# A hybrid encoder trunk on one core: four edits in the order of the first FFN

## The chip, the cores and the metric

The kernel runs on one core of one Trainium2 chip. A core has TensorE (matmuls; PE in the profile, with PEld for its weight loads), VectorE (DVE), ScalarE (ACT), GpSimd (POOL) and SyncE (SP, which issues transfers). TensorE reads its operands from on-chip memory (SBUF) and writes to accumulator banks (PSUM); a bank has to be read out before it is used again. The metric is the device time in microseconds (us) of one execution. The time before is 2467.57 us, the median of 3 runs (2467.53 to 2467.99).

## The reference, cut to what matters

Two layers, each a half-step FFN, a mixer (short convolution and attention) and a second half-step FFN, on 640 tokens of width 1024; all in float32.

```python
def _rmsnorm(x, g):
    y = xf * lax.rsqrt(jnp.mean(xf * xf, axis=-1, keepdims=True) + EPS)
    return y * g

def _swiglu(h, w_gu, w_down):              # w_gu: 1024 x 5632, w_down: 2816 x 1024
    g, u = jnp.split(h @ w_gu, 2, axis=-1)
    return (jax.nn.silu(g) * u) @ w_down

for l in range(2):
    x = x + 0.5 * _swiglu(_rmsnorm(x, norm_ffn1[l]), w_ffn1_gu[l], w_ffn1_down[l])
    x = x + mixer(_rmsnorm(x, norm_mix[l]))
    x = x + 0.5 * _swiglu(_rmsnorm(x, norm_ffn2[l]), w_ffn2_gu[l], w_ffn2_down[l])
```

The change touches only the first FFN of the first layer ("a0" in the code).

## The kernel before, in words

Everything is kept transposed: x is eight tiles of 128 channels by 640 tokens, and a matmul takes 128 x 128 weights and 320 tokens (one half of the tokens, `t1` or `t2`). To keep float32 accuracy with the faster matmul type, every operand is split into a high part (`hi`, made by ScalarE as a cast to fp32r) and a low part (`lo` = value - hi, made by VectorE), and a product is three matmuls: hi x hi, lo x hi (of x) and hi x lo (of the weights). So each slab of weights (128 x 1024, tile `raw`) costs one cast on ScalarE (L369, `whi`) and one subtraction on VectorE (L375, `wlo`).

The norm's scale per token is not applied to x ahead of the products. The matmuls run on x times the gain; the sum of squares of x is built meanwhile (`square` on ScalarE, `add` on VectorE), summed over the channels by TensorE (`begun`, L552), turned into a root on ScalarE (L742) and spread over the partitions by TensorE again (`spread`, L571), which gives `rho`; the results of the products are multiplied by `rho` when they are read out of their banks.

**The opening** (`opening`, L755 on). The first four columns of gates are computed plainly: eight products `po` (gate and up of columns 0 to 3), eight blocks of x deep. For the first two products the loop over k (L770) brings in x block by block: `ex.plain(k)` splits x's block (for even k in two halves, L677 to L680; for odd k in one go, L668 and L669), and L774 and L775 split the piece of the first two weight slabs that has just landed. The two products fill two accumulators; there are only two such accumulators (each two banks), so the third product waits until the first is read out by `out(0)`, a copy on ScalarE (L795), and the fourth until `out(1)` (L803). A loop of eight squares and additions (L813) follows the matmuls in the text, and the two copies stand in it behind the fifth and the sixth square. Temporary tiles (squares, g and u) share four buffers.

**Seven products for four** (`gate_up`, L895 on). The later columns use sums and differences of weights and of x so that seven block products do the work of eight. A gate has four slabs s0 to s3; s1 is a sum that VectorE makes first (`source`, two additions on L298, then L369 and L375 split it). The closing work of a gate (`tail`, L1029) multiplies the gate by rho, makes the product g * u (`Pair.product`, L1059), splits it (`parts`) and so makes an operand for a later down product. It is put into a list and run later, at the place where the next unit calls it.

**The down products by rows** (`down_rows`, L1159 on). After gates 4 and 5 comes the first group of the down product of columns 0 to 3: accumulators A (for a and, in its second half of life, its sums), B and two single banks c. Seven matmul groups (`mul`) follow one another, and results are read out by `stage` (a copy on ScalarE, sent to x by an accumulating transfer on POOL, `send`) or by `take` (VectorE adds the bank to x, L1202). The last group (XT4) accumulates into A on top of what `take(a, ...)` has read, so it waits for that. In this first group the tail of gate 5 and the step "d1" (`place`, the three sums L1133 to L1136 of `Pair.rest`) stand near the start, ahead of the first `take`.

**The order.** From the start up to gate 6 the order on TensorE, VectorE and ScalarE is that of the text, written out by hand (`order(ORDERED)`, L1298); from gate 6 (L1304) only TensorE's is, and the scheduler may put work of VectorE and ScalarE from there into holes that it sees ahead. Transfers of weight slabs are issued on SP (L294); POOL issues some weight loans (`lent`, L277 and L278) and the accumulating transfers to x (L1197).

Of the kernel before, what the change touches and what calls it, by code (L numbers as in the profile page):

```python
# [12 lines left out]
AF = mybir.ActivationFunctionType  # L13
# [3 lines left out]
P = 128  # L17
# [169 lines left out]
def two(ps):  # L187
    return ps[:, :, :HT]


def halves(t):
    return t.rearrange("p (a b) -> p a b", a=2)
# [3 lines left out]
def trunk(ctx: ExitStack, tc: tile.TileContext, xin, wst, small, pbias, samplebias, kcache, vcache, gfin,  # L196
          yout, yrows, ko, vo, co):
    nc = tc.nc
    PE, DVE, ACT, POOL, SP = nc.tensor, nc.vector, nc.scalar, nc.gpsimd, nc.sync
# [21 lines left out]
    def acc(name):  # L221
        return banks["acc"].tile([P, 2, 512], F32, tag="acc", name=name)

    def att(name):
        return banks["att"].tile([P, 512], F32, tag="att", name=name)
# [4 lines left out]
    def tmp(name):  # L230
        return tp.tile([P, UW], F32, tag="t", name=name)[:, :T]
# [27 lines left out]
    raws, ready = [], []  # L259
# [113 lines left out]
    def flush(n=None):  # L373
        for lo, src, hi in pending[:n]:
            DVE.tensor_tensor(out=lo, in0=src, in1=hi.bitcast(F32), op=ALU.subtract)  # L375
        del pending[:n]
# [20 lines left out]
    def ahead():  # L397

        source(len(ready))
# [41 lines left out]
    def multiply(ps, ws, xs, first, last, seeded=False):  # L441
        (wh, wl), (xh, xl) = ws, xs
        for j, (w, x) in enumerate(((wh, xh), (wh, xl), (wl, xh))):
            for a in range(2):
                PE.matmul(ps[:, a, :HT], w, x[a] if isinstance(x, tuple) else x[:, a * HT : (a + 1) * HT],  # L445
                          start=first and j == 0 and not seeded, stop=last and j == 2,
                          skip_group_check=seeded)
# [43 lines left out]
    x = [xp.tile([P, T], F32, name=f"x{k}") for k in range(KT)]  # L491
    for k in range(KT):
# [4 lines left out]
        c = slice(k // 2 * 2 * P, (k // 2 + 1) * 2 * P)  # L497
# [86 lines left out]
    class Expand(Stats):  # L584
# [71 lines left out]
        def plain(self, m):  # L656

            kp, odd = divmod(m, 2)
            n = f"{self.name}_{kp}"
            g = sm[:, self.goff + m : self.goff + m + 1]  # L660

            def low(lo, src, hi):
                DVE.scalar_tensor_tensor(out=lo, in0=src, scalar=g, in1=hi.bitcast(F32),
                                         op0=ALU.mult, op1=ALU.subtract)

            if odd:
                hi, lo = (z[:, 3:5] for z in self.ops[kp])
                ACT.activation(hi, halves(x[m]), AF.Copy, scale=g)  # L668
                low(lo, halves(x[m]), hi)  # L669
                return tuple(tuple(z[:, a] for a in range(2)) for z in (hi, lo))  # L670
            hi, lo = (self.fp.tile([P, 7, HT], F32R, name=f"x{i}{n}", tag=f"x{i}{kp}") for i in ("hi", "lo"))
            self.ops.append((hi, lo))
            if kp % 2 == 0:
                self.side = [hp.tile([P, T], F32R, tag=f"h{i}", name=f"x2{i}{n}") for i in ("hi", "lo")]
            c = slice(kp % 2 * HT, (kp % 2 + 1) * HT)
            out = (hi[:, X11], self.side[0][:, c]), (lo[:, X11], self.side[1][:, c])
            for a, (h, l) in enumerate(zip(*out)):  # L677
                src = x[m][:, a * HT : (a + 1) * HT]
                ACT.activation(h, src, AF.Copy, scale=g)
                low(l, src, h)  # L680
            return out
# [73 lines left out]
    def opening(fp, name, goff, n, pairs, tails):  # L755

        ACT.copy(early, epst)
        ex = Expand(fp, name, goff)  # L760
        h = []
        for i in range(2):
            ready.append(tuple(wp.tile([P, CH], F32R, tag=f"w{t}", name=f"w{t}{i}", bufs=3) for t in ("hi", "lo")))

        idle, row = att("idle"), tmp("row")[:, :P]
        DVE.memset(row, 1.0)
        for i in range(WAKE):
            PE.matmul(idle[:, :P], ones.to_broadcast([P, P]), row, start=i == 0, stop=i == WAKE - 1)
        first = [acc(f"po{name}_{i}") for i in range(2)]
        for k in range(KT):  # L770
            h.append(ex.plain(k))
            c = slice(k // 2 * 2 * P, (k // 2 + 1) * 2 * P)
            raw, (whi, wlo) = raws[k % 2], ready[k % 2]
            ACT.copy(whi[:, c], raw[:, c])  # L774
            DVE.tensor_tensor(out=wlo[:, c], in0=raw[:, c], in1=whi[:, c].bitcast(F32), op=ALU.subtract)  # L775
            if k % 2:
                for p, w in zip(first, ready):
                    for kk in (k - 1, k):
                        multiply(p, [z[:, kk * P : (kk + 1) * P] for z in w], h[kk], kk == 0, kk == KT - 1)
        used[0] = 2  # L780

        mixed = [z for kp in range(NP) for z in [ex.mixed(kp)] * 2]
        made = {2: (0,), 3: (1, 2, 3), 4: (4,), 5: (5, 6), 6: (7,)}
        us, gs, ps = [], [], first

        def out(i):

            j, up = divmod(i, 2)
            if not up:
                gs.append(tmp(f"g{name}_{j}"))  # L790
                if j:
                    scaled(gs[j], ps[i], ex.rho)
                    ACT.activation(gs[j], gs[j], AF.Silu)
                else:
                    ACT.copy(halves(gs[j]), two(ps[i]))  # L795
                return
            u = tmp(f"u{name}_{j}") if j > 1 else fp.tile([P, T], F32, tag="cap", name=f"u{name}_{j}", bufs=6)
            us.append(u)
            if j:
                scaled(u, ps[i], ex.rho)  # L800
                DVE.tensor_tensor(out=u, in0=u, in1=gs[j], op=ALU.mult)
            else:
                ACT.copy(halves(u), two(ps[i]))  # L803

        def begun():
            ex.total(att(f"nps{name}"))
            ex.root()
            ex.diagonal()

        at = {2: {6: begun}, 3: {1: lambda: ex.spread([att(f"nbc{name}_{a}")[:, :HT] for a in range(2)])}}  # L810
        prep(2)
        flush()
        for k in range(KT):  # L813
            ex.square(k)
            ex.add()
            if k in (4, 5):
                out(k - 4)
        for i in range(2, 2 * n):
            ps.append(acc(f"po{name}_{i}"))
            product(ps[i], h, at.get(i, {}))  # L820
            if i > 2:
                out(i - 1)
            if i == 3:
                g, u = gs[0], us[0]
                DVE.tensor_tensor(out=g, in0=g, in1=ex.rho, op=ALU.mult)
                ACT.activation(g, g, AF.Silu)
                DVE.tensor_tensor(out=u, in0=u, in1=ex.rho, op=ALU.mult)
            flush()
            for m in made.get(i, ()):
                next(mixed[m])  # L830
            if i == 3:
                DVE.tensor_tensor(out=u, in0=u, in1=g, op=ALU.mult)
            if i == 4:
                pairs[0].even(us[0])
            if i == 5:
                pairs[0].odd(us[1])
            if i == max(made):
                ahead()
                ex.flush()
                pairs[0].mixed()  # L840
                pairs[0].fourth()()
            if i == 2 * n - 1:
                pairs[1].even(us[2])
        ahead()
        out(2 * n - 1)
        tails += [lambda: pairs[1].odd(us[3]), pairs[1].mixed, pairs[1].fourth]
        ex.rest = None
        return ex
# [201 lines left out]
    class Pair:  # L1050
# [72 lines left out]
        def low(self, lo, hi, z):  # L1123
            DVE.tensor_tensor(out=lo, in0=z, in1=hi.bitcast(F32), op=ALU.subtract)
# [34 lines left out]
    def down_rows(fp, n, ms, pairs, tails, later, sent):  # L1159
# [4 lines left out]
        c = [att(f"dc{n}_{u}")[:, :HT] for u in range(2)]  # L1164
        t1, t2 = slice(0, HT), slice(HT, T)
        second = ms[0] > 0
# [11 lines left out]
        def place(name):  # L1178
            step(later, f"r{int(second)}{name}")

        def tail():
            for t in tails:
                t(False)
            tails.clear()
# [10 lines left out]
        def send(z, r, cols):  # L1195
            for u in range(2):
                POOL.dma_start(x[ms[2 * u + r]][:, cols], z[:, u], accum_op=ALU.add)  # L1197
# [11 lines left out]
        behind.clear()  # L1209
        prep(used[0] + 1)  # L1210
        begin()
        if not second:
            tail()
        flush()
        place("d1")
        mul(b, s0, 1, X21, True)
        with soon():
            take(b, 0, t1)
# [11 lines left out]
        with soon():  # L1230
            take(a, 1, t2, -0.5)
        send(c5, 1, t2)
        flush()
        ahead()
        mul(c, s2, 1, X22, False)
# [923 lines left out]
    class Final:  # L2159
# [145 lines left out]
        def out(self, k, rr):  # L2305
            z = x[k][:, :FEAT]
            DVE.scalar_tensor_tensor(out=z, in0=z, scalar=sm[:, O_GF + k : O_GF + k + 1],
                                     in1=rr, op0=ALU.mult, op1=ALU.mult)
            SP.dma_start(yout[:, k], z)
# [170 lines left out]
```

## Time and profile before

| what | us |
|---|---|
| median of 3 runs | 2467.57 |
| the profiled execution | 2468.21 |
| its span (first to last instruction) | 2466.4 |
| TensorE busy in the span | 2458.3 |
| VectorE busy | 2196.8 |
| ScalarE busy | 1396.9 |
| GpSimd busy | 329.7 |

Times inside the execution are counted from the start of the span. A row of the timeline is: start, duration, engine, line of the kernel, operation, tile written <- tiles read, shape, xN when N like instructions in a row are merged, and in brackets the idle time of the engine ahead of it with what ended it. A row of the waits is: who waited <- for whom, total, times, longest. A row of the stretches is: the stretch, its length, then for each of PE, PEld, DVE, ACT and POOL the busy time and (xN) the instructions, the granted clock, the share of the DMA engines and GB/s. A row of a group has its busy time and the mean duration of one in ns behind the bar. The granted TensorE clock is 1.00 in the whole span.

### The profile page before, as it was taken

To read this page: it belongs to the slowest core of one execution; us is meant where nothing else is said; L and a number is where in the kernel's file an instruction comes from. 1 tells how busy PE (TensorE), PEld (TensorE's weight loads), DVE (VectorE), ACT (ScalarE), POOL (GpSimd) and SP (SyncE) were. 2 spreads that over 40 slices of the span, in tenths; PEclk is the share of its full clock that TensorE was granted. 3 is DMA by queue.
4 is the path that set the end of the run, shared out by engine and by line. 5 is a ranking of instruction groups with operands and counts; after the bars stand their busy time and mean duration, and the time that the engine had idled before them with its cause. 6 is when DMAs were issued, how large, how long until landed. Compare 5 with 4: busy or idle time off the path is not lost.

```text
span 2466.4 us, 44136 instructions
## 1 busy us (share of the span) xinstructions
PE 2458.3 (100%) x17234; PEld 2409.1 (98%) x17234; DVE 2196.8 (89%) x3725; ACT 1396.9 (57%) x2246; POOL 329.7 (13%) x495
## 2 busy tenths in 40 slices
PE   9999999999999999999999999999999999999999
PEld 9999999889999999999999999998899999999998
DVE  7999999888998899998799999988889979999997
ACT  6555556665655555555665555566656556555555
POOL 0211112211110001011001111121110000111111
PEclk9999999999999999999999999999999999999999
DMA  4553444335443334445334343453454433444444
GB/s 156 138 126 100 121 118 122 111 112 175 116 130 123 87 102 112 108 118 123 107 97 109 109 119 101 118 129 102 139 160 122 122 115 94 108 113 107 113 118 118
DMA packets 115282, 290.93 MB, mean 118 GB/s; under 512 B 13216, under 2 KB 53664, under 8 KB 115072
## 3 DMA queue, kind: packets, MB, share of 16 engines
q1 hardware_dynamic: 69840, 220.10, 28.3%
q0 software_dynamic: 44800, 67.75, 14.6%
q8 instruction: 135, 2.21, 0.4%
q14 instruction: 75, 0.61, 0.1%
q10 hardware_dynamic: 432, 0.25, 0.0%
HBM read 241.57 MB, written 7.94 MB: 101 GB/s over the span
## 4 chain that ended last, share of the span: by engine, by line
PE 97%; DMA 1%; DVE 1%; ACT 0%; issue 0%; SPq 0%; DVEq 0%; ACTq 0%
PE pab L469 13%; PE paa L469 11%; PE pcb L469 6%; PE pca L469 6%; PE daa L1175 6%; PE dab L1175 5%; PE po L445 5%; PE qa L469 4%; PE pbb L469 3%; PE pba L469 3%; PE dca L1175 3%; PE dcb L1175 3%; PE ma_qk L469 2%; PE ma_cv L469 2%; PE pv L1872 2%; PE qc L469 2%
## 5 line engine op out<-in xcount | busy, mean ns | idle before, releaser
L369 ACT CAST whi<-raw 128x1024 fp32r<-128x1024 f32 (+1 forms) x564 | 500.1, 892 | 376.1 <-DVE raw L298 63.6
L375 DVE TENSOR_TENSOR wlo<-raw,whi 128x1024 fp32r<-128x1024 f32 (+1 forms) x602 | 580.0, 967 | 135.4 <-ACT whi L369 131.8
L369 ACT CAST whi<-s 128x1024 fp32r<-128x1024 f32 (+1 forms) x166 | 155.2, 935 | 287.3 <-issue 111.3
L469 PE MATMUL pab<-xhib,whi 128*128 128x320 f32 x704 | 217.5, 309 | 0.0
L469 PE MATMUL pab<-xhib,wlo 128*128 128x320 f32 x704 | 217.0, 308 | 0.0
L469 PE MATMUL pab<-xlob,whi 128*128 128x320 f32 x704 | 217.0, 308 | 0.0
L469 PE MATMUL paa<-xhia,whi 128*128 128x320 f32 x640 | 197.7, 309 | 0.0
L469 PE MATMUL paa<-xloa,whi 128*128 128x320 f32 x640 | 197.5, 309 | 0.0
L469 PE MATMUL paa<-xhia,wlo 128*128 128x320 f32 x640 | 197.4, 308 | 0.0
L375 DVE TENSOR_TENSOR wlo<-s,whi 128x1024 fp32r<-128x1024 f32 (+1 forms) x169 | 179.1, 1060 | 3.6 <-ACT whi L369 3.6
L1197 POOL DMA_DIRECT2D x<-c_a x80 | 70.0, 1014 | 568.3 <-ACT ahia L1076 244.8
L1197 POOL DMA_DIRECT2D x<-c_b x72 | 63.1, 1009 | 582.2 <-ACT ahib L1076 205.8
L469 PEld LDWEIGHTS pab<-xhib,whi 128*128 128x128 f32 x704 | 132.1, 188 | 0.9 <-issue 0.9
L469 PEld LDWEIGHTS pab<-xlob,whi 128*128 128x128 f32 x704 | 132.2, 188 | 0.0
L469 PEld LDWEIGHTS pab<-xhib,wlo 128*128 128x128 f32 x704 | 132.1, 188 | 0.0
L469 PEld LDWEIGHTS paa<-xhia,whi 128*128 128x128 f32 x640 | 120.1, 188 | 0.6 <-issue 0.4
L469 PEld LDWEIGHTS paa<-xloa,whi 128*128 128x128 f32 x640 | 120.2, 188 | 0.2 <-DVE xloa L712 0.2
L469 PEld LDWEIGHTS paa<-xhia,wlo 128*128 128x128 f32 x640 | 120.1, 188 | 0.0
L298 DVE TENSOR_TENSOR raw<-s,raw 128x512 f32<-128x512 f32 x166 | 113.1, 682 | 0.0
L469 PE MATMUL pcb<-xhib,wlo 128*128 128x320 f32 x352 | 108.7, 309 | 0.0
L469 PE MATMUL pcb<-xlob,whi 128*128 128x320 f32 x352 | 108.5, 308 | 0.0
L469 PE MATMUL pcb<-xhib,whi 128*128 128x320 f32 x352 | 108.5, 308 | 0.0
(896 smaller groups left out, 8248.3 us busy)
## 6 DMA issues: line engine op xcount, KB each, us to landing
raw<-in_wst SPq DMA_DIRECT2D x374, 512.0 KB, 3.7
x<-c_a POOLq DMA_DIRECT2D x80, 160.0 KB, 4.4
x<-c_b POOLq DMA_DIRECT2D x72, 160.0 KB, 3.5
one<-in_wst POOLq DMA_DIRECT2D x40, 256.0 KB, 3.5
lent<-in_wst POOLq DMA_DIRECT2D x36, 256.0 KB, 3.8
kc<-in_kcache SPq DMA_DIRECT2D x32, 256.0 KB, 5.0
vc<-in_vcache SPq DMA_DIRECT2D x16, 512.0 KB, 4.6
x<-u_a POOLq DMA_DIRECT2D x40, 160.0 KB, 4.3
```

Source lines behind the costliest of these rows:

```text
L298: DVE.tensor_tensor(out=out, in0=a, in1=b, op=op)
L369: ACT.copy(hi[:, d], src[:, c])
L375: DVE.tensor_tensor(out=lo, in0=src, in1=hi.bitcast(F32), op=ALU.subtract)
L445: PE.matmul(ps[:, a, :HT], w, x[a] if isinstance(x, tuple) else x[:, a * HT : (a + 1) * HT], start=first and j == 0 and not seeded, stop=l ...
L469: PE.matmul(ps, a, b, start=start and kp == 0 and j == 0, stop=stop and kp == NP - 1 and j == 2, skip_group_check=True)
L1175: PE.matmul(ps[u], w, y, start=start and i == 0 and j == 0, stop=i == 1 and j == 2, skip_group_check=True)
L1197: POOL.dma_start(x[ms[2 * u + r]][:, cols], z[:, u], accum_op=ALU.add)
L1872: PE.matmul(pv[t], xx[:, t * P : (t + 1) * P], w[:, kk * AW : (kk + 1) * AW], start=c == 0 and kk == 0 and j == 0, stop=c == KT // 2 - 1 a ...
```

## The change

Four edits, all in the first FFN of the first layer:

- in `plain`, x's block 1 is split in its two token halves instead of in one go: two casts and two subtractions of 320 in place of one each of 640;
- in `opening`, the first piece of the first weight slab is cast by VectorE, ahead of the loop, instead of by ScalarE;
- `out(0)` and `out(1)`, the copies of the first two accumulators, stand behind the third and the fourth square instead of behind the fifth and the sixth;
- in the first group of `down_rows` of columns 0 to 3 (`sent` is true and `second` false), the tail of gate 5 and the step "d1" stand behind `take(a, 1, t2, -0.5)` and its `send` instead of ahead of the second group of matmuls.

```diff
             if odd:
                 hi, lo = (z[:, 3:5] for z in self.ops[kp])
-                ACT.activation(hi, halves(x[m]), AF.Copy, scale=g)
-                low(lo, halves(x[m]), hi)
+                for c in (slice(0, 1), slice(1, 2)) if m == 1 else (slice(0, 2),):
+                    ACT.activation(hi[:, c], halves(x[m])[:, c], AF.Copy, scale=g)
+                    low(lo[:, c], halves(x[m])[:, c], hi[:, c])
...
         first = [acc(f"po{name}_{i}") for i in range(2)]
+        c = slice(0, 2 * P)
+        DVE.tensor_copy(ready[0][0][:, c], raws[0][:, c])
         for k in range(KT):
             h.append(ex.plain(k))
             c = slice(k // 2 * 2 * P, (k // 2 + 1) * 2 * P)
             raw, (whi, wlo) = raws[k % 2], ready[k % 2]
-            ACT.copy(whi[:, c], raw[:, c])
+            if k:
+                ACT.copy(whi[:, c], raw[:, c])
             DVE.tensor_tensor(out=wlo[:, c], in0=raw[:, c], in1=whi[:, c].bitcast(F32), op=ALU.subtract)
...
         for k in range(KT):
             ex.square(k)
             ex.add()
-            if k in (4, 5):
-                out(k - 4)
+            if k in (2, 3):
+                out(k - 2)
...
         begin()
-        if not second:
+        put_off = sent and not second
+        if not second and not put_off:
             tail()
         flush()
-        place("d1")
+        if not put_off:
+            place("d1")
         mul(b, s0, 1, X21, True)
...
         send(c5, 1, t2)
+        if put_off:
+            tail()
+            place("d1")
         flush()
         ahead()
         mul(c, s2, 1, X22, False)
```

## The prediction

> **What bounds the kernel now.** I read the busy shares first, then the waits by PE over the whole run, because a wait on the engine that is always busy is the only place where time can be won.
>
> ```profile
> PE 2458.3 (100%) x17234; PEld 2409.1 (98%) x17234; DVE 2196.8 (89%) x3725; ACT 1396.9 (57%) x2246; POOL 329.7 (13%) x495
> ...
> PE poa L445 <- ACT ga L795: 0.7, 1, 0.7
> PE poa L445 <- DVE xloa L663: 0.3, 1, 0.3
> ```
>
> TensorE is the bound, and its waits that have a name are all in the first FFN, under 1 us each. Every edit of the change aims at one of them, so the size of the whole matter is about 2 us in 2468. Next I read the timelines of the engines around each wait. The opening comes first, across engines:
>
> ```profile
> 6.44 0.88 DVE L663 SCALAR_TENSOR_TENSOR xloa<-x,sm,xhia 128x640 fp32r<-128x640 f32 x1 [0.22 <-ACT xhia L668]
> ...
> 7.38 0.56 PE L445 MATMUL poa<-xloa,whi 128*128 128x320 f32 x2 [0.26 <-DVE xloa L663]
> ...
> 8.07 0.31 PE L445 MATMUL poa<-xhia,whi 128*128 128x320 f32 x1
> ...
> L1962 DVE COPY pt<-ptp 128x256 f32<-128x256 f32 x12 | 4.5, 412 | 0.0
> ```
>
> The pair of matmuls at 7.38 starts 0.06 us after the low half of x's second block (6.44 + 0.88 = 7.32): up to 8.07 TensorE follows VectorE. Then the end of the two first banks, on ScalarE, VectorE and TensorE:
>
> ```profile
> 16.36 1.05 ACT L369 CAST whi<-raw 128x1024 fp32r<-128x1024 f32 x1 [0.40 <-DMA raw<-in_wst]
> 17.96 2.61 ACT L731 ACTIVATE sqa<-x 128x640 f32<-128x640 f32 x4
> 18.71 6.41 DVE L298 TENSOR_TENSOR ssuma<-ssuma,sqa 128x640 f32<-128x640 f32 x7
> 20.47 0.67 ACT L795 COPY ga<-poa 128x640 f32<-128x640 f32 x1
> 21.19 0.41 PE L445 MATMUL poa<-xhia,whi 128*128 128x320 f32 x1 [0.65 <-ACT ga L795]
> 25.53 1.28 ACT L742 ACT_TABLE_LOAD   x1
> 26.67 0.51 PE L552 MATMUL npsa<-ones,ssuma 128*32 128x1 f32 x40
> 27.27 0.27 ACT L742 ACTIVATE nrmsa<-npsa,epst 128x5 f32<-128x5 f32 x1 [0.46 <-PE npsa L552]
> 32.11 0.82 DVE L582 TENSOR_TENSOR ga<-poa,rhoa 128x640 f32<-128x640 f32 x1 [2.12 <-ACT rhoa L579]
> ```
>
> The wait at 21.19 is for the copy of a bank. The root of the norm (27.27) follows TensorE's sums, and VectorE stands until rho is there (32.11). What comes after is the point on which most of the forecast rests:
>
> ```profile
> DVE ga L582 <- ACT rhoa L579: 2.1, 1, 2.1
> DVE xloa L712 <- ACT xhia L706: 1.3, 2, 0.7
> DVE eloa L1124 <- ACT ehia L1093: 0.5, 1, 0.5
> ...
> 53.00:79.60 26.60, 26.60 (x183) 26.60 (x182) 26.23 (x42) 12.12 (x20) 1.43 (x2) 1.00 0.23 60
> ...
> 78.92 1.05 ACT L369 CAST whi<-s 128x1024 fp32r<-128x1024 f32 x1 [5.32 <-DVE s L298]
> ...
> 80.51 0.41 ACT L985 COPY c_a<-paa 128x320 f32<-128x320 f32 x1
> 80.97 0.42 PE L469 MATMUL paa<-xhia,whi 128*128 128x320 f32 x1
> ```
>
> The first three lines are all that VectorE waits for between 32.5 and 79 (the first is the wait that ends with rho): ScalarE alone, never TensorE or a DMA. The row of the stretch 53 to 79.6 has VectorE busy 26.23 of 26.60 us. At its end ScalarE's cast waits for VectorE's sums, the copy of c1 stands behind that cast, and TensorE starts 0.05 us after the copy (80.51 + 0.41 = 80.92). So at 80.97 TensorE is not ahead of VectorE and ScalarE any more, and they have run since rho at a pace of their own.
>
> **The change part by part.** *First weights by VectorE, x's second block in halves.* Removed: one cast on ScalarE; added: one copy on VectorE, and one more ScalarE and one more VectorE instruction. The copy stands in VectorE's queue ahead of the low halves. No row has it from SBUF; by the bounds it costs VectorE between nothing (it fits before x's first low half) and 0.41 us (the COPY row, from PSUM), and I take 0.3. The halves let one matmul of the pair at 7.38 begin some 0.4 earlier, the other not. Together the start at 8.07 moves between 0.4 later (the copy's whole price) and 0.4 earlier (the copy free, both matmuls as early as the first); I take 0.1 earlier. How little hangs on it the next two steps show.
>
> *Banks copied two squares earlier.* Nothing is added on ScalarE; two copies change places with squares. Four squares take 2.61, so 0.63 each from one to the next: squares two and three start at 17.96 and 18.59, and the first copy at 19.22. It ends at 19.22 + 0.67 = 19.89, when TensorE is still in its last matmuls (they end 0.65 before 21.19, at 20.54). Matmuls start every 0.145 (26.60 us for 183 of them in the stretch row) and one lasts 0.31, so the next could start at 20.54 - 0.31 + 0.145 = 20.38. Today it starts at 21.19, and the first one after a stop lasts 0.41 instead of 0.31: 0.81 + 0.1 = 0.9 us are won here. The squares behind the copies come 0.57 to 1.2 later, but the last one ends as before, and VectorE's seven additions end at about 25.4 instead of 18.71 + 6.41 = 25.12. The sums on TensorE then start at 26.67 - 0.9 - 0.1 = 25.7, still behind the additions. If that cover were gone, it would cost 0.3.
>
> Now what is late next. The root waits for two things: the sums, then done at 26.2, and the table load on its own engine, which ends at 25.53 + 1.28 = 26.81. That load stands behind the same squares, copies and casts as before, and these behind a transfer that the change doesn't touch (16.36). So the root comes 0.46 earlier at most, less some 0.02: 0.44, not 1.0. Everything behind rho moves by this 0.44 and TensorE meets it again at 80.97. **These three edits give -0.44**, between 0 (the root is held by the additions after all) and -0.46. [...]
>
> *The gate tail behind an evacuation.* The rows, on VectorE, ScalarE and TensorE:
>
> ```profile
> 93.23 0.82 DVE L1032 TENSOR_TENSOR ga<-ga,rhoa 128x640 f32<-128x640 f32 x1 [0.42 <-ACT ga L1019]
> 94.09 0.82 DVE L1069 TENSOR_TENSOR doa<-ua,ga 128x640 f32<-128x640 f32 x1
> ...
> 96.64 0.81 DVE L1124 TENSOR_TENSOR aloa<-doa,ahia 128x640 fp32r<-128x640 f32 x1
> 98.56 0.31 PE L1175 MATMUL daa<-thia,wlo 128*128 128x320 f32 x1
> 98.91 0.48 DVE L1136 TENSOR_TENSOR doa<-doa,dea 128x320 f32<-128x320 f32 x1
> 99.31 0.88 DVE L1202 SCALAR_TENSOR_TENSOR x<-dba,x 128x320 f32<-128x320 f32 x2
> 100.11 0.88 DVE L1202 SCALAR_TENSOR_TENSOR x<-daa,x 128x320 f32<-128x320 f32 x2
> 100.91 1.28 DVE L375 TENSOR_TENSOR wlo<-raw,whi 128x512 fp32r<-128x512 f32 x2
> 100.61 0.31 PE L469 MATMUL paa<-xloa,whi 128*128 128x320 f32 x1
> 101.04 0.42 PE L1175 MATMUL daa<-t4hia,whi 128*128 128x320 f32 x1
> 102.11 0.68 DVE L298 TENSOR_TENSOR s<-raw 128x512 f32<-128x512 f32 x1
> 103.63 1.05 ACT L369 CAST whi<-s 128x1024 fp32r<-128x1024 f32 x1 [5.11 <-DVE s L298]
> 104.83 1.22 DVE L375 TENSOR_TENSOR wlo<-s,whi 128x1024 fp32r<-128x1024 f32 x1
> 106.43 0.31 PE L469 MATMUL paa<-xhia,wlo 128*128 128x320 f32 x1
> 115.64 0.89 POOL L278 DMA_DIRECT2D lent<-in_wst  x1 [7.28 <-DMA lent<-in_wst]
> 127.38 0.62 ACT L369 CAST whi<-lent 128x512 fp32r<-128x512 f32 x1
> ```
>
> The order is written out by hand for these three engines, so I can lay VectorE's queue anew. TensorE's group at 101.04 waits for the evacuation at 100.11, which stands behind the tail. With the tail behind it, the evacuation waits only for the matmul of 98.56, which ends at 98.87. TensorE loses 101.04 - 100.61 - 0.145 = 0.28 here today, and 0.1 of restart; this 0.39 is won.
>
> What is queued behind the evacuation: instructions of VectorE overlap by 0.08 (98.91 + 0.48 against 99.31). The tail is 0.86 (to 94.09) + 0.74 + 0.73, and the three sums of "d1" are 3 x 0.40 and 0.1 for one that waits on another, together 3.65. Without them the evacuation of 99.31 starts at about 95.7 and ends 0.8 later, so VectorE stands from 96.4 until 98.87. Only then come this 3.65; the low halves of the next slab, 1.20; and only then the sums that start at 102.11. The next instruction after the evacuation issues between 98.87 + 0.40 (its first half went while the second was computed) and 98.87 + 0.80. So the sums start at 104.1 to 104.5, 2.0 to 2.4 later than 102.11, and with them the cast of 103.63 and the low half of 104.83, which ends at 108.05 to 108.45. Who waits: TensorE's matmul at 106.43 needs that low half, which today ends 0.38 before it (104.83 + 1.22 = 106.05). It starts at 108.1 to 108.5, with a restart of 0.1. Against 106.43 that is +1.8 to +2.2 with the 0.39 already in; **I take +1.9**. The cast is on the path too (it ends at 104.1 + 1.52 + 1.05 = 106.7, for the matmul two before, due at 106.43 - 0.29 - 0.39 = 105.75), but the low half ends last. ScalarE's own part of the tail, one cast, fits its idle 5.11. On POOL the later sends and the loan of weights behind them slide by the same 2 us; the loan of 115.64 is read at 127.38, so that is covered by 10 us, and the loads on SP by the late TensorE itself.
>
> The sum against the profiled execution: 2468.21 us, of which the span is 2466.4 and 1.8 lie around it. -0.44 + 1.9 = +1.46, so 2469.7 for such an execution. It was 0.64 above the median 2467.57, so the median becomes **2469.0**.
>
> **The rivals.** *A, the tail does what it is for, faster:* the sums of 102.11 don't come late, because VectorE gets work done in its 2.5 us of standing, so the 0.39 is won: -0.44 - 0.39 = -0.83, 2466.7. It decides from sums that start before 102.5 (0.38 of slack). For it speaks that the tail's 3.65 would mostly fit into that hole, if the compiled order puts some of it there; against it, that the sums are behind the tail in the text and that ScalarE's copy at 80.51 shows a queue standing behind one waiting instruction. [...]
>
> *B, all of TensorE's waits are won:* 0.9 and 0.1 in the opening, 0.39 at 101, so -1.4, 2466.2. It needs VectorE and ScalarE ahead of TensorE at 80.97, and the 26.23 of 26.60 speaks against it.
>
> *C, the change does nothing it says:* the copy lands in a temporary buffer that a square needs, the root comes when it did, and the tail's loss and gain cancel: 2467.6.
>
> *D, worse by the same mechanism:* one more low half of 0.73 (as at 96.64) that today runs ahead of the evacuation stays behind the tail as well: +0.7 on the forecast, 2469.7.
>
> **How the numbers follow.** Forecast 0.52, A 0.26, B 0.07, C 0.07, D 0.08. From 2466.4 to 2470.0 all but B is held; the likeliest case alone runs from 2467.57 - 0.46 + 1.8 - 0.3 = 2468.6 to 2467.57 + 0 + 2.2 = 2469.8. What a measurement can tell from no change is 0.2%, 4.9 us; no case reaches it, so no change has 0.97, 0.01 and 0.02 are for what I don't see.
>
> **What would show it.** After the change: no wait for ga L795 near 20.5; the root directly behind its table load; TensorE's start of c1's next group near 80.5, 0.44 earlier; no wait before the matmuls of t4 near 100; and a new wait of TensorE near 105 to 108, for whi or wlo from s, of 1.9 to 2.2 in all. The forecast is wrong if that last wait is missing (A), and its first part is wrong if the group of 80.97 starts more than 0.6 earlier (B).

## The result, and the profile after

| kernel | median, us | runs | ratio to before (95% interval) |
|---|---|---|---|
| before, beside the change | 2467.73 | 19 | |
| after | 2472.09 (2470.6 to 2473.6) | 19 | 1.0016 (1.0009 to 1.0023) |

The changed kernel is slower by 4.4 us, or 0.18%, where +1.5 was forecast, and 2.1 us above the top of the range. Its profiled execution took 2470.6 us (span 2468.8), the shortest of its 19; the times lie in three groups, near 2470.9 (six runs), 2472.2 (ten) and 2473.3 (three). Both matter below.

The opening first. The lines are picked from the timeline of the changed kernel, across engines:

```profile
15.97 1.05 ACT L369 CAST whi<-raw 128x1024 fp32r<-128x1024 f32 x1 [0.39 <-DMA raw<-in_wst]
...
20.20 0.31 PE L445 MATMUL poa<-xhia,whi 128*128 128x320 f32 x1
20.39 0.69 ACT L807 COPY ua<-poa 128x640 f32<-128x640 f32 x1 [0.26 <-PE poa L445]
...
25.52 1.28 ACT L743 ACT_TABLE_LOAD   x1
26.82 0.27 ACT L743 ACTIVATE nrmsa<-npsa,epst 128x5 f32<-128x5 f32 x1
...
80.06 0.41 ACT L989 COPY c_a<-paa 128x320 f32<-128x320 f32 x1
80.52 0.41 PE L469 MATMUL paa<-xhia,whi 128*128 128x320 f32 x1
```

The third product starts at 20.20 without a wait, the root follows its table load at once, and TensorE meets c1 at 80.52 where it had been 80.97. That is 0.45, just what the forecast's -0.44 asks for, and yet it is mostly not owed to the change: by the first line the third slab landed 0.39 earlier than in the profile of before (cast at 15.97, there 16.36). And ScalarE has a wait that it did not have, 0.26 us for TensorE ahead of the second copy (L807).

Next VectorE, ScalarE and TensorE around the moved tail, from the timeline of the same kernel (picked rows: of TensorE's matmuls only those next to t4 and to the stop):

```profile
98.51 0.89 DVE L1206 SCALAR_TENSOR_TENSOR x<-daa,x 128x320 f32<-128x320 f32 x2 [2.54 <-PE daa L1179]
99.31 0.81 DVE L1036 TENSOR_TENSOR ga<-ga,rhoa 128x640 f32<-128x640 f32 x1
99.85 0.31 PE L1179 MATMUL dca<-ohia,wlo 128*128 128x320 f32 x1
100.00 0.31 PE L1179 MATMUL daa<-t4hia,whi 128*128 128x320 f32 x1
...
103.25 0.82 DVE L1128 TENSOR_TENSOR aloa<-dea,ahia 128x640 fp32r<-128x640 f32 x1
...
104.79 0.68 DVE L298 TENSOR_TENSOR s<-raw 128x512 f32<-128x512 f32 x1
105.13 0.31 PE L469 MATMUL pba<-xhia,wlo 128*128 128x320 f32 x1
106.30 1.04 ACT L369 CAST whi<-s 128x1024 fp32r<-128x1024 f32 x1 [3.93 <-DVE s L298]
107.25 0.70 ACT L1193 ACTIVATE t_a<-daa 128x640 f32<-128x640 f32 x1
107.51 1.22 DVE L375 TENSOR_TENSOR wlo<-s,whi 128x1024 fp32r<-128x1024 f32 x1
107.85 0.42 ACT L989 COPY c_a<-paa 128x320 f32<-128x320 f32 x1
108.32 0.42 PE L469 MATMUL paa<-xhia,whi 128*128 128x320 f32 x1 [2.88 <-ACT c_a L989]
...
108.78 0.41 PE L469 MATMUL paa<-xhia,wlo 128*128 128x320 f32 x1
```

VectorE stands for 2.54 us ahead of the evacuation, as foreseen. The group of t4 (100.00) starts without a wait. The sums come at 104.79, and TensorE, which has nothing to do after 105.13, stands for 2.88 us. The two things that let it go end 0.46 apart: the copy of c1 on ScalarE at 108.27, then the low half on VectorE at 108.73, for which the matmul of 108.78 waits.

### The profile page after: what moved, and what is told of

Read it like the earlier page. It is cut to its first block, busy times and chain, and to the rows that moved or that the text cites. A ratio compares the mean times of both kernels' runs of the same rounds, so it can differ in the third digit from the quotient of the medians.

```text
span 2468.8 us, 44136 instructions
## 1 busy us (share of the span) xinstructions
PE 2458.9 (100%) x17234; PEld 2409.0 (98%) x17234; DVE 2197.7 (89%) x3727; ACT 1397.1 (57%) x2246; POOL 329.6 (13%) x495
## 4 chain that ended last, share of the span: by engine, by line
PE 99%; DVE 0%; DMA 0%; issue 0%; ACT 0%; DVEq 0%; ACTq 0%
PE pab L469 13%; PE paa L469 11%; PE pcb L469 6%; PE pca L469 6%; PE daa L1179 6%; PE dab L1179 5%; PE po L445 5%; PE qa L469 4%; PE pbb L469 3%; PE pba L469 3%; PE dca L1179 3%; PE dcb L1179 3%; PE poa L445 2%; PE ma_cv L469 2%; PE ma_qk L469 2%; PE pv L1881 2%
```

## The experiments

All runs of a comparison shared the runs of the kernel before. None of the kernels leaves work out; one adds some.

| kernel | median, us | before beside it | ratio (95% interval) |
|---|---|---|---|
| opening_only | 2468.08 | 2467.43 | 1.0002 (0.9993 to 1.0011) |
| tail_only | 2471.82 | 2467.43 | 1.0019 (1.0010 to 1.0028) |
| mended | 2467.48 | 2467.43 | 1.0000 (0.9991 to 1.0009) |
| after_again | 2472.54 | 2467.43 | 1.0021 (1.0012 to 1.0030) |
| before_again | 2467.68 | 2467.74 | 1.0000 (0.9991 to 1.0009) |
| banks_only | 2468.18 | 2467.74 | 1.0002 (0.9994 to 1.0011) |
| start_only | 2467.93 | 2467.74 | 1.0002 (0.9993 to 1.0011) |
| mended_tail_only | 2467.70 | 2467.74 | 1.0000 (0.9991 to 1.0008) |
| x21_twice | 2470.82 | 2467.77 | 1.0013 (1.0004 to 1.0022) |
| held_early | 2471.54 | 2467.77 | 1.0013 (1.0004 to 1.0023) |
| copies_apart | 2467.63 | 2467.77 | 0.9999 (0.9990 to 1.0008) |
| copies_apart_mended_tail | 2467.29 | 2467.77 | 0.9998 (0.9989 to 1.0007) |

**Which part costs the time.** `opening_only` has the first three edits with the tail where it was; `tail_only` is the kernel before with the fourth alone.

```diff
 # opening_only, on the changed kernel
-        put_off = sent and not second
+        put_off = False
```

> The three edits of the opening, with the tail of gate 5 back where it was. Theory 1 (all of the loss comes from the tail): 0.4 us below the kernel before, about 2467.3 against 2467.73, the group of 80.97 at 80.5, the wait of 0.28 ahead of the t4 matmuls still there, and executions as close together as before. Rival (the opening has a part in the loss): at or above the time before.

```diff
 # tail_only, on the kernel before
+        put_off = sent and not second
-        if not second:
+        if not second and not put_off:
             tail()
...
+        if put_off:
+            tail()
+            place("d1")
         flush()
```

> The moved tail alone. Theory 1: a wait of TensorE of about 3.0 us ahead of the third group of gate 6, so a span 2.8 above the kernel before in its best executions, about 2470.5, and the same scatter up to 3 us above it as the changed kernel has, so a median near 2472.5. Rival: with the opening as it was the scatter is gone and the median is at 2470.5 or below.

`tail_only` carries the whole loss (+4.39 us), with the same TensorE wait of 2.9 us for c1. `opening_only` gives nothing that can be measured: +0.65 between the medians, and an interval that holds 1. The -0.44 does not show in the median. In its trace, where the third slab's cast began at 16.36 as in the first trace of before, the copy of c1 began at 80.22 in place of 80.51 and the span is 2466.1 in place of 2466.4: with the same landing, 0.29 of the 0.44 is there.

**The changed kernel once more,** for a second trace.

> The changed kernel once more, for a trace of another execution. Theory 2 (the scatter is the clock: the stop of 3 us in some executions makes the granted clock fall): an execution above 2471.5 shows a granted clock below 1.00 in the stretch right behind the stop and matmuls at twice their spacing there, and nothing else differs. Rival (the scatter is transfers or something along the whole span): the clock is 1.00 behind the stop and the time is lost in other places.

It took 2472.54, and its profiled execution 2473.49. The stretches are cut so that its clock changes at borders (107.84 and 114.66); the columns are the stretch, its length, busy time and (instructions) of PE, PEld, DVE, ACT and POOL, the granted clock, the share of the DMA engines and GB/s:

```profile
104.43:107.84 3.41, 1.29 (x9) 1.03 (x8) 3.38 (x8) 1.25 (x2) 0.58 (x2) 1.00 0.50 77
107.84:111.25 3.41, 2.64 (x10) 2.64 (x11) 3.32 (x6) 2.27 (x5) 3.41 (x5) 0.50 0.77 124
111.25:114.66 3.41, 3.41 (x15) 3.41 (x14) 1.44 (x3) 0.43 (x1) 0.10 (x1) 0.50 1.06 208
114.66:118.08 3.42, 3.42 (x25) 3.42 (x25) 1.99 (x3) 1.37 (x2) 0.00 (x0) 1.00 0.67 247
```

The timeline of TensorE in the same execution:

```profile
105.42 0.31 PE L469 MATMUL pba<-xhia,wlo 128*128 128x320 f32 x1
108.61 0.64 PE L469 MATMUL paa<-xhia,whi 128*128 128x320 f32 x1 [2.88 <-ACT c_a L989]
...
109.31 0.47 PE L469 MATMUL paa<-xhia,wlo 128*128 128x320 f32 x1
109.58 0.47 PE L469 MATMUL paa<-xhia,whi 128*128 128x320 f32 x1
```

The stop is as long as in the first trace, 2.88 us. But behind it the granted clock is 0.50 for two stretches of 3.41 us, and in them matmuls start every 0.267 us and not every 0.147. From the first matmul behind the stop to the 25th, 6.35 us pass here and 3.79 in the first trace: the half clock costs 2.6 us. The rest of the 2.9 between the two executions is mostly the later start (the last matmul ahead of the stop at 105.42, there 105.13). In the first trace the clock does not fall behind the stop:

```profile
103.24:106.65 3.41, 2.20 (x15) 1.93 (x14) 3.38 (x8) 0.35 (x1) 0.00 (x1) 1.00 0.50 79
106.65:110.07 3.42, 1.75 (x11) 1.59 (x12) 3.33 (x6) 3.18 (x6) 3.10 (x5) 1.00 0.51 83
```

The stop of 2.88 us (105.44 to 108.32) lies in these two stretches of the changed kernel's first trace, and the clock is 1.00 in both and in the one behind them (110.07 to 113.48). What tells this execution from the other is not shown. `tail_only` had the third outcome, one stretch at half clock:

```profile
104.56:107.97 3.41, 0.90 (x7) 0.64 (x5) 3.38 (x7) 1.64 (x3) 0.97 (x2) 1.00 0.37 63
107.97:111.39 3.42, 3.04 (x11) 3.04 (x12) 3.33 (x6) 1.88 (x5) 3.12 (x4) 0.50 0.91 142
```

Counted in the same way (4.98 us from the first to the 25th matmul behind the stop, for 3.79) that costs 1.2 us. From 111.39 to 114.80 the clock is 1.00 again. Starting from the shortest execution, no drop, one and two would put the executions near 2470.6, 2471.8 and 2473.2, close to the three groups of the result (2470.9, 2472.2 and 2473.3). Each of the three outcomes was traced once in kernels with this stop; that every execution of a group had its number of drops is inferred from the times.

**Is it the clock?** `x21_twice` is the changed kernel with one product of gate 6 computed twice, so that TensorE has work in the stop; everything else stays in its order.

```diff
-            mul(pb, s0, 1, X21, every, True, True)
+            for _ in range(2 if n == "a0_6" else 1):
+                mul(pb, s0, 1, X21, every, True, True)
```

> The changed kernel, but the first gate group behind the first down rows computes its product X21 twice (12 matmuls more, the second pass starts the bank anew, so the sum is the same). Nothing else moves on any engine. TensorE stood from 105.13 to 108.32 in the changed kernel; the 12 matmuls at 0.147 us fill 1.76 us of it, so it stands only from about 107.04 to 108.32, and the work behind starts when it did. Theory (the stop of 3.2 us makes TensorE's clock fall to half for one or two stretches of 3.41 us in most executions, which costs 1.2 to 2.9 us): the clock stays at 1.0 behind 108, and the median falls to that of the executions without the drop, 2470.6 (2470.2 to 2471.0), although TensorE does more work. Rival (the scatter of the changed kernel comes from elsewhere, the landing of the third slab for one): the median stays at 2472.1 to 2472.5, with single times up to 2473.5.

The median is 2470.82, and nine of the eleven runs lie between 2470.6 and 2471.3. Twelve matmuls more made the kernel 1.3 to 1.7 us faster than the changed kernel. The intervals of the ratios overlap, but the single times differ clearly: of the changed kernel's 30 runs six were below 2471.4, of these eleven nine. The timeline of TensorE in that kernel, and two stretches of 3.41 us:

```profile
107.01 0.31 PE L469 MATMUL pba<-xhia,wlo 128*128 128x320 f32 x1
108.45 0.42 PE L469 MATMUL paa<-xhia,whi 128*128 128x320 f32 x1 [1.12 <-ACT c_a L989]
```

```profile
104.57:107.98 3.41, 2.75 (x19) 2.49 (x17) 3.38 (x8) 1.55 (x3) 0.89 (x2) 1.00 0.48 77
107.98:111.39 3.41, 2.94 (x19) 2.79 (x20) 3.31 (x6) 2.40 (x6) 3.21 (x4) 1.00 0.88 139
```

The work behind the stop of 1.12 us starts when it did (108.45), and the clock stays at 1.00. This tells the clock from the stop itself: the clock costs some 1.3 to 1.7 us of the median, the rest of the loss stays. Two runs were at 2472.4 and 2472.6; no trace shows why.

**What made the stop 2.9 long and not 1.9.** `held_early` calls the held half of the pair's first product (the row of 103.25 above, and its copy on ScalarE) ahead of the second group, where VectorE stands idle.

```diff
         s1 = slab(True)[0]
         flush()
+        if put_off:
+            for t in held:
+                t()
+            held.clear()
         mul(a, s1, 0, XN6, False)
```

> The changed kernel, but the held product's copy and low half (ScalarE 0.73 us, VectorE 0.82 us) are called ahead of the second down group, in VectorE's hole of 2.54 us ahead of 98.5, in place of behind the tail; each of the two engines has this one instruction at another place and nothing else. Theory (that low half is 0.82 us of the stretch ahead of the sums): the sums begin at about 103.97 in place of 104.79, the copy of the first weights, the stage and the copy of c1 all 0.82 earlier, and TensorE stands from 105.13 to about 107.5, 2.4 start to start. If a stop of that length leaves the clock alone, the median is 2469.8; if the clock still falls in most executions, 2471.3. Rival (ScalarE's own queue or the first weights' landing sets the stop, not that half): the stop stays at 3.2 and the time at 2472.

The timeline of that kernel, VectorE and TensorE, and its stretches ahead of the fall of the clock (107.92) and behind it:

```profile
95.90 0.82 DVE L1128 TENSOR_TENSOR aloa<-dea,ahia 128x640 fp32r<-128x640 f32 x1
...
104.19 0.68 DVE L298 TENSOR_TENSOR s<-raw 128x512 f32<-128x512 f32 x1
...
107.73 0.48 PE L469 MATMUL paa<-xhia,whi 128*128 128x320 f32 x1 [2.27 <-ACT c_a L989]
```

```profile
104.51:107.92 3.41, 1.14 (x8) 0.88 (x7) 3.38 (x6) 2.21 (x4) 1.54 (x3) 1.00 0.41 73
107.92:111.34 3.42, 3.42 (x14) 3.31 (x14) 3.29 (x7) 1.39 (x4) 2.55 (x4) 0.50 1.13 162
```

The half fits the hole, the sums come 0.60 earlier (104.19 for 104.79), and the stop shrinks by 0.61 (2.27 for 2.88). It is 0.60 and not 0.82 for two reasons: from its start to the next instruction's the half takes only 0.73 (103.25 to 103.98), and the two sums that it had stood between, the second of which reads the first, start 0.52 apart without it (102.86 and 103.38), 0.12 more than the 0.40 from such a sum to the instruction behind it. The clock falls all the same, behind a stop of 2.27 us: median 2471.54, three of eleven runs at 2470.0 to 2470.6.

**The tail at another place.** In `mended` (an edit of the changed kernel; `tail` hands the list on to the product) the put-off product stands ahead of the group XT7, and its split and "d1" at the end of the down group, behind the next weights; `mended_tail_only` has this without the first three edits.

```diff
+        parts = []
         if second:
             tail()
+        elif put_off:
+            tail(parts)
         mul(a, s2, 0, XT7, False)
...
-        if put_off:
-            tail()
-            place("d1")
         flush()
         ahead()
...
         flush()
+        if put_off:
+            for t in parts:
+                t()
+            place("d1")
```

> The opening as changed; the gate product of the tail stands ahead of the evacuation take(a), in the time in which VectorE stands, and its split and the three sums of d1 behind the last weights of the group. Theory 1 (the sums for the next slab came late because 3.65 us of tail stood ahead of them): no long wait in gate 6, no wait at t4 or a short one, 0.4 to 0.8 below the kernel before, 2466.9 to 2467.3, with little scatter. Rival (any tail behind the first evacuation makes TensorE wait): 1 us or more above the kernel before.

> The opening as it was before, the gate product of the tail ahead of take(a), and its split and d1 behind the last weights of the group. Theory: the 0.39 at the t4 matmuls is won and nothing lost, 2467.05 against 2467.43 of the kernel before. Rival: the new order costs what it wins, 2467.4 or above.

The timeline of `mended`, VectorE and the first matmul of t4 (of the lines that show the product, the sums and the matmul):

```profile
96.09 0.82 DVE L1036 TENSOR_TENSOR ga<-ga,rhoa 128x640 f32<-128x640 f32 x1
96.94 0.82 DVE L1073 TENSOR_TENSOR doa<-ua,ga 128x640 f32<-128x640 f32 x1
...
100.30 0.68 DVE L298 TENSOR_TENSOR s<-raw 128x512 f32<-128x512 f32 x1
100.50 0.36 PE L1179 MATMUL daa<-t4hia,whi 128*128 128x320 f32 x1
```

The product lies in the hole, the sums come 4.5 us earlier than in the changed kernel, and the stop is gone (2467.48). So the place ahead of the sums is what costs, not the tail's work. Neither kernel gains measurably on the one before, where some 0.4 or more was expected: +0.05 and -0.04.

**The opening, edit by edit.** `before_again` is the kernel before once more; `start_only` has the halves and VectorE's cast; `banks_only` the bank copies alone.

> The kernel before against itself, for the scatter of the measure and for the trace of another execution. Theory 3 (the start of the record decides some tenths: when the first whole slab lands differs between executions, and the root of the norm follows it): the interval holds 1.0000, and the cast of the third slab, at 16.36 in the first trace, starts anywhere from 15.9 to 16.4, the copy of c1 at 80.51 moving with it. Rival: that cast is at 16.36 as before, and the executions differ at another place.

```diff
 # start_only, on the changed kernel, with put_off = False
-            if k in (2, 3):
-                out(k - 2)
+            if k in (4, 5):
+                out(k - 4)
```

> The first weights cast by VectorE and x's second block in halves, and nothing else. By my forecast within 0.1 of the kernel before. If the 0.65 comes from here, 2468.0 or above; then TensorE's start of the third product should be later than with the copies alone.

```diff
 # banks_only, on the kernel before
-            if k in (4, 5):
-                out(k - 4)
+            if k in (2, 3):
+                out(k - 2)
```

> The two copies behind the third and fourth square, and nothing else. If the copies give what I forecast, 0.3 to 0.45 below the kernel before, 2467.0 to 2467.15. If the 0.65 that the three edits of the opening cost together in the median comes from here, 2468.0 or above.

The medians (-0.06, +0.44 and +0.19) don't tell which edit the +0.65 of `opening_only` comes from: each interval spans some 2 us on either side. The traces tell more. ScalarE's timelines, of `before_again` and then of `banks_only`:

```profile
15.95 1.05 ACT L369 CAST whi<-raw 128x1024 fp32r<-128x1024 f32 x1 [0.39 <-DMA raw<-in_wst]
...
25.11 1.28 ACT L742 ACT_TABLE_LOAD   x1
26.86 0.27 ACT L742 ACTIVATE nrmsa<-npsa,epst 128x5 f32<-128x5 f32 x1 [0.47 <-PE npsa L552]
...
80.11 0.41 ACT L985 COPY c_a<-paa 128x320 f32<-128x320 f32 x1
```

```profile
16.22 1.05 ACT L369 CAST whi<-raw 128x1024 fp32r<-128x1024 f32 x1 [0.40 <-DMA raw<-in_wst]
...
20.65 0.69 ACT L803 COPY ua<-poa 128x640 f32<-128x640 f32 x1 [0.26 <-PE poa L445]
...
25.77 1.28 ACT L742 ACT_TABLE_LOAD   x1
27.07 0.27 ACT L742 ACTIVATE nrmsa<-npsa,epst 128x5 f32<-128x5 f32 x1
...
80.30 0.41 ACT L985 COPY c_a<-paa 128x320 f32<-128x320 f32 x1
```

The kernel before is a rigid chain from the third slab's cast to the copy of c1: 80.51 - 16.36 = 64.15 in its first trace and 80.11 - 15.95 = 64.16 here. With the banks copied early it is 80.30 - 16.22 = 64.08, in the changed kernel 64.09, and in `after_again`, where the slab landed at 16.45, 63.89. Over all seven traces with this edit it lies between 63.86 (`opening_only`, cast at 16.36) and 64.20 (`x21_twice`, cast at 15.96, where the second copy waited for 0.40). So the edit gains between nothing and 0.29, least where the slab lands earliest: the second copy stands in ScalarE's queue ahead of four squares, two casts and the table load, and waits there for the end of product 1, which does not move with that slab.

`copies_apart` checks this by putting the second copy one square later, where its bank is done.

```diff
 # copies_apart, on the kernel before
-            if k in (4, 5):
-                out(k - 4)
+            if k in (2, 4):
+                out(k // 2 - 1)
```

> The kernel before, but the first banks are copied behind the third and the fifth square (the change: third and fourth). Theory (behind the fourth square the second copy comes before TensorE has ended product 1, so it waits 0.26 us and ties the table load and the root to that end; behind the fifth the bank is done): ScalarE does not wait for TensorE from the first square to the table load, the load ends 10.45 us behind the third slab's first cast whenever that lands, the root stands right behind it, and the copy of c1 near 80.5 begins 63.7 us behind that cast in place of 64.17. Time 2467.3 if no later wait takes the 0.45 back, 2467.4 if a wait of 0.13 near 370 comes with it. Rival (what the opening gains is taken up at later waits, of which the change's trace shows small ones at 43 to 77): c1 at 64.1 and the time within 0.15 of the kernel before.

Its timeline of ScalarE:

```profile
16.49 1.05 ACT L369 CAST whi<-raw 128x1024 fp32r<-128x1024 f32 x1 [0.40 <-DMA raw<-in_wst]
...
21.19 0.68 ACT L803 COPY ua<-poa 128x640 f32<-128x640 f32 x1
...
25.67 1.28 ACT L742 ACT_TABLE_LOAD   x1
26.96 0.27 ACT L742 ACTIVATE nrmsa<-npsa,epst 128x5 f32<-128x5 f32 x1
...
80.19 0.41 ACT L985 COPY c_a<-paa 128x320 f32<-128x320 f32 x1
```

No wait at the second copy, the load ends 10.46 behind the cast, the root directly behind it, and c1 63.70 behind the cast: the 0.45 is there in the trace. The median is only 0.14 below the kernel before. Part of the difference is a new stop of 0.15 us on TensorE near 370, which is in the traces of the changed kernel, `held_early`, `x21_twice`, `opening_only`, `banks_only` and `copies_apart`, and not in `mended` or the last kernel below. In `banks_only` the matmul behind it starts at 369.90, 0.05 after ScalarE's copy of a bank (L1005) ends; in `before_again` that copy ended 0.29 ahead of the matmul. Why ScalarE is late there stays open. The rest is under what the intervals can tell.

**Both repairs in one:** the banks behind the third and the fifth square, the tail as in `mended`.

> Both in one: the banks copied behind the third and the fifth square, and the tail's product ahead of the second group's third product with its split and the pair's rows at the end of that group. Theory: the gain of the copies (0.45) and of the tail (the wait of 0.39 at t4 gone, no new stop near 105) add up: 2467.0 to 2467.2. Rival (what is won ahead of the second down group and the later gate groups is taken back by the order of the work behind): 2467.6 to 2467.8, no difference from the kernel before.

2467.29 against 2467.77. Its trace ends 0.60 us earlier than that of `before_again` though its slab landed 0.25 later (16.20), which makes 0.85, near the 0.45 + 0.39 that the two waits were said to be worth. The interval of the ratio holds 1: it is the lowest median of all, and not shown to be faster.

## Why the prediction was wrong, step by step

**Right: the sign, the place and the mechanism of the moved tail.** No wait at t4, VectorE standing from 96.0 to 98.5, the tail and "d1" ahead of the sums, and a new stop between 105 and 109 that ends with the copy of c1 and the low half of the sums. A fell: nothing passed the evacuation, ahead of which VectorE stood for 2.54 us.

**Wrong in size: "I take +1.9".** The sums were due 2.0 to 2.4 later than 102.11, so with the opening's 0.44 taken off at 103.7 to 104.1; they came at 104.79. The 3.65 us laid behind the evacuation left out the held low half, which stood in the same stretch before and stayed in it. That was rival D, priced 0.7 and given 0.08; `held_early` shows 0.60 for it. It should have been in the sum from the start, since it ran between the sums of "d1" in the kernel before too, as this row of VectorE's timeline there shows, ahead of the sum of 98.91:

```profile
97.78 0.81 DVE L1124 TENSOR_TENSOR aloa<-dea,ahia 128x640 fp32r<-128x640 f32 x1
```

The rest, 0.1 to 0.5, is that the whole evacuation went first (98.51 to 99.31; the upper bound taken was the right one). The matmul that had started at 106.43 starts at 108.78; with 0.45 of earlier arrival that is +2.8. A restart costs twice 0.1, at 108.32 (0.42 for 0.31) and at 108.78 (0.41), since c1 and the low half let TensorE go one after the other. That c1 stands on ScalarE behind the cast and the stage was not foreseen, but cost little: the low half ends 0.46 after it.

**The step that failed: that a stop costs what it lasts.** The forecast, and rival D with it, went from a stop of 2 us to a loss of 2 us; no rival had a cost behind the stop in it. More was lost here: the granted clock fell to 0.50 behind the stop, for 3.42 us in one trace (`tail_only`) and for 6.82 in another (`after_again`), which cost 1.2 and 2.6 us, and by their times most executions had such a drop. That accounts for the three groups between 2470.6 and 2473.6, and `x21_twice` ties it to TensorE's standing: with a stop of 1.12 us in place of 2.88 the clock stayed at 1.00 in the trace, and the median is 1.3 lower. The executions that look free of a drop (2470.6 to 2471.0) are still 0.6 or more above the top of the range, by the stop's size.

**"These three edits give -0.44": not kept.** The gain hung on one execution. There TensorE waited 0.65 us for the first copy; in `before_again`, with the slab 0.41 earlier, the waits of TensorE have no such line. The step said nothing of the second copy: it became the next thing on ScalarE's way, and the gain at c1 was between nothing and 0.29, with 0.15 given back near 370. "The last one ends as before" is where it failed: that holds only when the second copy finds its bank done, and it waited 0.26 us in the changed kernel. The bound by the table load (1.28 us long) was right; in every trace with the early copies the root stands within 0.02 us of it.

**The start edits** did about what was said: the matmul of 8.07 began at 7.89 to 8.16 in the seven traces with them (the middle one 8.01) and at 8.07 to 8.55 in the seven without (8.22), some 0.2 earlier where 0.1 was taken, and nothing of it shows at the end (`start_only` +0.19, interval around 1).

**A reading that was off, without effect.** Not all named waits of TensorE were under 1 us: the waits of the kernel before also have one of 1.1 us at the very start (`idle`, L768, for POOL), which no edit touches.

The sum of the medians, +4.4, in these terms: +1.46 forecast, +0.9 by which the stop was undersized (2.8 for 1.9), +0.4 for the opening that gave nothing, +0.1 near 370, and +1.3 for the clock (2472.1 against the 2470.8 of `x21_twice`), 4.2 in all. The 0.2 that is left is below what these medians can tell.

## What to carry to other kernels

A stop of the bounding engine is to be priced with what follows it: here a stop of 2.88 us cost nothing, 1.2 or 2.6 us more in clock, and filling it with 1.76 us of matmuls whose result was not needed took 1.3 us off the median. Taking the stop away, as `mended` does, is better still. When an instruction is moved behind one that waits, write out everything that stands between it and the next thing that the bounding engine needs, held work included, and ask whether the hole ahead of the wait can take it. A gain of 0.4 us that is read from one execution needs a second one, to see what part of it came with a transfer's landing.

## What the runs showed of the hardware that was not expected

**Behind the stop the clock fell to half for 3.4 or 6.8 us.** In three traces it was 0.50 behind the stop: from 107.84 to 114.66 (`after_again`), from 107.97 to 111.39 (`tail_only`) and from 107.92 to 111.34 (`held_early`), which is 6.82, 3.42 and 3.42 us. In the 3.41 us ahead of the fall TensorE had been busy for 1.29, 0.90 and 1.14 us. In `after_again` the first matmul behind the stop came 0.77 us after the fall (108.61), in `held_early` 0.19 ahead of it (107.73). Behind the same stop of 2.88 us the clock stayed at 1.00 in the changed kernel's first trace, and behind the 1.12 us of `x21_twice` too. At the end of the execution, where TensorE runs out of work, the clock fell 2.0 us behind its last matmul in the changed kernel (2463.25, the fall at 2465.26) and 5.3 in the kernel before (2460.87 and 2466.19). So in these traces the length of a stop alone does not say whether the clock falls behind it, nor for how long; what decides it is not shown.

**One slab's landing sets the opening.** The third slab's cast began between 15.90 and 17.25 us from execution to execution, in kernels whose edits do not touch that transfer, and in the five traces with the bank copies where they were before, the copy of c1 near 80.5 followed it at 64.15 to 64.19.
